# Moving one stream of weight loads from SyncE's queue to GpSimd's

## The chip, the cores and the metric

The kernel runs on one core of a Trainium2 chip. A core has engines that run their own instruction streams and meet at semaphores: TensorE (PE in the profile; its weight loads are PEld), VectorE (DVE), ScalarE (ACT), GpSimd (POOL) and SyncE (SP), which here does nothing but issue DMAs. A DMA is issued by an engine's queue and carried out by the core's 16 DMA engines. The metric is device time in microseconds of one execution; each version is given as the median of several runs.

## The reference

The program is a small backbone of two layers over 256 latent tokens and 256 context tokens of width 1024, batch 1. Each layer has a half-step SwiGLU, a mixer (neighbourhood attention in layer 0, a short gated convolution in layer 1) and another half-step SwiGLU. Every sub-layer is modulated by vectors that are computed from a conditioning vector:

```python
for i in range(DEPTH):
    m = (s_c @ ada_w[i] + ada_b[i]).reshape(B, N_MOD, 1, D)     # latent tokens
    mc = (s_cc @ ada_w[i] + ada_b[i]).reshape(N_MOD, D)         # context tokens
    x = half_step_ffn(x, m[:, 0], m[:, 1], m[:, 2], ffn_w_in[i, 0], ffn_w_out[i, 0], ...)
    if ctx_in:
        ctx = half_step_ffn(ctx, mc[0], mc[1], mc[2], ffn_w_in[i, 0], ffn_w_out[i, 0], ...)
    hx = modulate(x, m[:, 3], m[:, 4])
    ...
```

with `half_step_ffn` = LayerNorm(alpha x + 0.5 gate f(x (1 + scale) + shift)), f(h) = (silu(a) u) w_out, (a, u) = h w_in, and D_FF = 2816. `ada_w` has 2 x 1024 x 9216 fp32 numbers, 75 MB: nine blocks of 1024 x 1024 a layer, each of which gives one modulation vector from a vector-matrix product. These are the modulation weights.

## The kernel before

Everything is fp32. For TensorE each fp32 operand is split into a rounded high part and a low rest, and a product takes three matmuls (high x high, high x low, low x high). A unit of FFN weights comes into a raw buffer (`w1r` for the input matrix, `w2r` for the output matrix, tag `wr`, four buffers, issued by SyncE at L202), ScalarE rounds it into `w1h` or `w2h` (L207) and VectorE subtracts to get `w1l` or `w2l` (L210). Each split goes in two halves. A raw buffer is free again when VectorE's second half is done.

Three stages matter here.

1. **Start** (to about 46 us). The first two modulation blocks, needed at once, are loaded through SyncE (`start_load`, L577) and multiplied on TensorE, while the first inputs come.
2. **First FFN** (about 46 to 401 us), for latent and context tokens together. It goes in three parts over the hidden width (4, 4 and 3 panels). In each, `f0_mm` makes the chunks of the hidden layer (TensorE L671), `f0_gate` takes silu on ScalarE (L680), multiplies on VectorE (`sil`, L681), rounds on ScalarE (`gh`, L109) and subtracts on VectorE (`gl`, L110); then `out_gemm` multiplies with w_out (TensorE L161, L162, L164).
3. **The rest**: attention, and from about 600 us the other FFNs and the convolution.

Beside the first FFN runs a **background stream**: 11 of the modulation blocks, in seven groups. The first three groups have one block each, used for two vectors (latent and context); the other four have two blocks each, used for one. The generator `ada` loads a block in eight pieces of 128 x 1024 (512 KB, tile `ar`, tag "ar", three buffers, L300), 88 in all, and VectorE accumulates each piece, times the conditioning value of its partition, in two halves into `acc` (L291 for the first piece of a block, L293 after that). So a piece costs four VectorE instructions in the first three groups and two in the others. Right after a piece is loaded its accumulation is traced. When a group's blocks are done, eight small matmuls with a matrix of ones sum over the partitions (L324), VectorE adds a bias (L325, from a tile that GpSimd clears once, L312, and SyncE loads, L315), and the rows go to a scratch in memory (L327).

`set_background` starts the stream with a rate; `tick`, called after every few matmuls as the program is traced, advances it by that rate, and `drain` (L763) finishes it at the end of the first FFN. Three more streams, set at L1095, L1098 and L1160, load the remaining modulation blocks through the same `ada` later, 40 pieces in all.

The order of TensorE's instructions is written by hand (`manual_schedule`). The order on the other engines is planned from priorities and readiness when the program is built; each engine then runs its instructions in that fixed order. An instruction waits, where it stands in its queue, for the semaphores that it needs: a load for its buffer, an accumulation for its load. What stands behind it in the same queue waits too. Before the change SyncE's queue holds all loads of the first FFN, weights and modulation pieces alike, and the small stores. GpSimd has clearing at the start, two small instructions a LayerNorm (L397, L398) and the additions of a bias to the attention mask (L872).

Of the kernel before, what the change touches and what calls it, by code (L numbers as in the profile page):

```python
# [16 lines left out]
P = 128  # L17
D = 1024
# [49 lines left out]
def backbone_kernel(  # L68
# [6 lines left out]
    nc = tc.nc  # L75
    sync = nc.sync
# [11 lines left out]
    w_early = [0]  # L88
    ext = [1, 0]
    ada_late = [0]  # L90

    def nm(s):
        uid[0] += 1
        return f"{s}_{uid[0]}"
# [10 lines left out]
    def tpb(s="tp"):  # L105
        return bank("tp", s)
# [28 lines left out]
    def bg_step():  # L135
        with tc.high_priority(offset=-ada_late[0]):
            if next(background[0], 0) == 0:
                background[0] = None
# [14 lines left out]
    def drain():  # L153
        while background[0] is not None:
            bg_step()
# [116 lines left out]
    def ada(vecs):  # L272


        acc = {}

        def accumulate(l, m, k, w):
            with ExitStack() as st:
                for i in gate_ins:
                    st.enter_context(tc.issue_after(i.ins))  # L280
                for i, vec in enumerate(vecs):
                    if vec[:2] != (l, m):
                        continue
                    if k == 0:
                        a = hp.tile([P, D], F32, tag="acc", bufs=2, name=nm("acc"))
                        acc[i] = [a[:, 0:512], a[:, 512:D]]
                    sc = cst[:, k, vec[2]:vec[2] + 1]
                    for h in range(2):
                        src, a = w[:, h * 512:(h + 1) * 512], acc[i][h]
                        if k == 0:  # L290
                            nc.vector.tensor_scalar(a, src, sc, None, op0=ALU.mult)  # L291
                        else:
                            nc.vector.scalar_tensor_tensor(out=a, in0=src, scalar=sc, in1=a,  # L293
                                                           op0=ALU.mult, op1=ALU.add)

        loaded = []
        for l, m in dict.fromkeys((l, m) for l, m, _ in vecs):
            for k in range(KC):
                w = hp.tile([P, D], F32, tag="ar", bufs=3, name=nm("ar"))
                sync.dma_start(w, ada_w[l, k * P:(k + 1) * P, m * D:(m + 1) * D])  # L300
                loaded.append((l, m, k, w))
                if len(loaded) > (ADA_LAG if gate_ins else 0):
                    accumulate(*loaded.pop(0))
                yield 1
        while loaded:
            accumulate(*loaded.pop(0))
            if loaded:
                yield 1
        n = 2 * len(vecs)
        if not bias_rows:  # L310
            bias_rows.append(hp.tile([P, 512], F32, tag="adab", name=nm("adab")))
            nc.gpsimd.memset(bias_rows[0], 0.0)  # L312
        bt = bias_rows[0]
        for i, (l, m, v) in enumerate(vecs):
            sync.dma_start(bt[64 * i:64 * i + 64:32], ada_b[l, m * D:(m + 1) * D].rearrange("(a b) -> a b", b=512))  # L315
        yield 1
        yield 1
        yield 1
        rows = hp.tile([P, 512], F32, tag="adar", name=nm("adar"))
        ps = tpb("ada")  # L320
        for i in range(len(vecs)):
            for h in range(2):
                j = 2 * i + h
                nc.tensor.matmul(ps[32 * j:32 * j + 32, :], ones, acc[i][h], start=True, stop=True)  # L324
        nc.vector.tensor_tensor(out=rows[:32 * n], in0=ps[:32 * n], in1=bt[:32 * n], op=ALU.add)  # L325
        for i, (l, m, v) in enumerate(vecs):
            sync.dma_start(scr[l][v, m * D:(m + 1) * D].rearrange("(a b) -> a b", b=512),  # L327
                           rows[64 * i:64 * i + 64:32, :])
        yield 1
# [3 lines left out]
    def stream(*groups):  # L333
        for g in groups:
            yield from ada(g)
            made[0] += 1
# [424 lines left out]
                     nk, order, evac, "w2", wrow0=k0 * P))  # L761

    drain()  # L763

    def s2t(s):
        return sp.tile([P, 512], F32, tag="s2", bufs=S2, name=nm(s))
# [345 lines left out]
    w = sc_w_in[0]  # L1112
# [103 lines left out]
```

## Time and profile before

| what | value |
|---|---|
| median of 3 runs | 1267.73 us (1265.61 to 1269.18) |
| the profiled execution's own time | 1268.98 us |
| its span, first to last instruction | 1267.2 us |
| mean granted TensorE clock | 0.997 |
| DMA, whole span | 268.59 MB, 212 GB/s |
| SyncE's queue (q1) | 267.48 MB, 67.4% of the 16 engines' time |
| DMA share, 46 to 176 us and 176 to 366 us | 0.73 and 0.78 |

The profile has one page and several views that can be cut to a stretch of time: busy time by stage, groups of instructions, who waited for whom and how long, one tile's instructions, and the timeline. In rows of groups and timelines stand the source line, the engine, the operation, what is written and read (names of tiles without buffer numbers), the shapes, the count, and in brackets or after a bar the idle time of the engine just before, with what ended it. "SPq" is SyncE's queue of issues. Times are microseconds from the start of the span, durations in groups nanoseconds.

### The profile page before, as it was taken

How to read it: one execution, taken by the hardware profiler on the slowest of the kernel's cores; microseconds unless marked ns; L12 is line 12 of the kernel's file. 1: busy time of each engine (PE TensorE's matmuls, PEld its weight loads, DVE VectorE, ACT ScalarE, POOL GpSimd, SP SyncE). 2: the span in 40 equal slices, each digit the busy share in tenths (PEclk: the TensorE clock that was granted, in tenths of full speed). 3: DMA queues.
4: the chain of work that ended last, by engine and by line, in shares of the span. 5: the costliest groups of instructions: out<-in, count | busy, mean ns of one | idle time of the engine just before them, and what ended most of it. 6: DMA issues, size and time to landing. Idle time of an engine off the chain costs nothing.

```text
span 1267.2 us, 17289 instructions
## 1 busy us (share of the span) xinstructions
PE 1245.2 (98%) x5910; PEld 1004.7 (79%) x5910; DVE 955.2 (75%) x1685; ACT 590.1 (47%) x1152; POOL 42.1 (3%) x71
## 2 busy tenths in 40 slices
PE   8999999999999999989999999999999999999997
PEld 5787778787778778767888788888788887888786
DVE  4698987588888867889898646988546788977546
ACT  2433132312326456687755535645435744655431
POOL 0000000000001111111000000000000000000000
PEclk9999999999999999999999999999999999999999
DMA  9977678497862654564899645898645764886641
GB/s 301 305 220 232 186 239 301 161 309 236 286 229 84 197 111 77 107 136 126 266 326 326 234 145 180 267 324 281 224 149 168 232 217 133 260 284 187 217 158 57
DMA packets 202776, 268.59 MB, mean 212 GB/s; under 512 B 30090, under 2 KB 149362, under 8 KB 202688
## 3 DMA queue, kind: packets, MB, share of 16 engines
q1 hardware_dynamic: 202652, 267.48, 67.4%
q8 instruction: 46, 0.75, 0.2%
q14 instruction: 42, 0.34, 0.1%
q10 hardware_dynamic: 36, 0.02, 0.0%
HBM read 265.27 MB, written 2.17 MB: 211 GB/s over the span
## 4 chain that ended last, share of the span: by engine, by line
PE 87%; DMA 4%; DVE 4%; ACT 3%; SPq 1%; issue 1%; POOL 0%; DVEq 0%; ACTq 0%; POOLq 0%
PE f L671 18%; PE w L161 17%; PE w L164 17%; PE w L162 17%; PE wc L161 2%; PE wc L164 2%; PE wc L162 2%; DMA ar<-in_ada_w_dram 2%; PE gT L482 1%; PE wkv L161 1%; PE wkv L162 1%; PE wkv L164 1%; PE S L956 1%; DMA bias<-in_na_rpb_dram 1%; PE wo L161 1%
## 5 line engine op out<-in xcount | busy, mean ns | idle before, releaser
L207 ACT ACTIVATE w1h<-w1r 128x512 fp32r<-128x512 f32 (+1 forms) x352 | 200.2, 620 | 173.7 <-PE w L164 68.4
L210 DVE TENSOR_TENSOR w1l<-w1r,w1h 128x512 fp32r<-128x512 f32 (+1 forms) x352 | 222.8, 678 | 46.7 <-ACT w1h L207 45.1
L161 PE MATMUL w<-w1h,hTh 128*128 128x512 f32 x528 | 209.4, 397 | 0.9 <-ACT hTh L109 0.9
L162 PE MATMUL w<-w1l,hTh 128*128 128x512 f32 x528 | 206.0, 390 | 0.2 <-DVE w1l L210 0.2
L293 DVE SCALAR_TENSOR_TENSOR acc<-ar,cst,acc 128x512 f32<-128x512 f32 x266 | 185.3, 745 | 14.6 <-DMA ar<-in_ada_w_dram 14.4
L161 PE MATMUL w<-w2h,gh 128*128 128x512 f32 (+1 forms) x446 | 173.5, 390 | 1.4 <-ACT gh L109 1.4
L162 PE MATMUL w<-w2l,gh 128*128 128x512 f32 (+1 forms) x446 | 172.1, 386 | 0.0
L210 DVE TENSOR_TENSOR w2l<-w2r,w2h 128x512 fp32r<-128x512 f32 x176 | 114.2, 687 | 72.6 <-ACT w2h L207 71.3
L207 ACT ACTIVATE w2h<-w2r 128x512 fp32r<-128x512 f32 x176 | 101.5, 624 | 144.3 <-PE w L164 105.7
L164 PE MATMUL w<-w1h,hTl 128*128 128x512 f32 x528 | 163.2, 390 | 0.3 <-DVE hTl L110 0.2
L671 PE MATMUL f<-h0h,w1h 128*128 128x512 f32 x352 | 137.2, 394 | 0.6 <-ACT w1h L207 0.6
L671 PE MATMUL f<-h0h,w1l 128*128 128x512 f32 x352 | 136.1, 390 | 1.1 <-DVE w1l L210 1.1
L164 PE MATMUL w<-w2h,gl 128*128 128x512 f32 (+1 forms) x446 | 136.2, 386 | 0.0
L671 PE MATMUL f<-h0l,w1h 128*128 128x512 f32 x352 | 136.1, 390 | 0.0
L161 PEld LDWEIGHTS w<-w1h,hTh 128*128 128x128 f32 x528 | 99.2, 188 | 23.8 <-ACT hTh L109 1.7
L164 PEld LDWEIGHTS w<-w1h,hTl 128*128 128x128 f32 x528 | 98.9, 188 | 22.4 <-DVE hTl L110 1.5
L162 PEld LDWEIGHTS w<-w1l,hTh 128*128 128x128 f32 x528 | 99.2, 188 | 20.2 <-DVE w1l L210 0.6
L161 PEld LDWEIGHTS w<-w2h,gh 128*128 128x128 f32 x446 | 83.8, 188 | 20.9 <-issue 2.5
L164 PEld LDWEIGHTS w<-w2h,gl 128*128 128x128 f32 x446 | 83.3, 188 | 17.2 <-DVE gl L110 0.2
L162 PEld LDWEIGHTS w<-w2l,gh 128*128 128x128 f32 x446 | 83.8, 188 | 16.6
L671 PEld LDWEIGHTS f<-h0h,w1h 128*128 128x128 f32 x352 | 65.8, 188 | 19.7 <-issue 5.0
L671 PEld LDWEIGHTS f<-h0h,w1l 128*128 128x128 f32 x352 | 65.9, 188 | 14.7 <-DVE w1l L210 1.6
(182 smaller groups left out, 1705.9 us busy)
## 6 DMA issues: line engine op xcount, KB each, us to landing
w1r<-in_ffn_w_in_dram SPq DMA_DIRECT2D x340, 256.0 KB
ar<-in_ada_w_dram SPq DMA_DIRECT2D x128, 512.0 KB
w2r<-in_ffn_w_out_dram SPq DMA_DIRECT2D x88, 512.0 KB
ar<-in_ada_w_dram SPq DMA_DIRECT2D x32, 256.0 KB
wkvr<-in_na_w_qkv_dram SPq DMA_DIRECT2D x32, 256.0 KB
wcr<-in_sc_w_in_dram SPq DMA_DIRECT2D x32, 256.0 KB
wqr<-in_na_w_qkv_dram SPq DMA_DIRECT2D x8, 512.0 KB
bias<-in_na_rpb_dram SPq DMA_DIRECT2D x64, 64.0 KB
```

The source lines that it names most:

```text
L161: nc.tensor.matmul(ps, lh, rh, start=first and i == 0, stop=False)
L162: nc.tensor.matmul(ps, lh, rl, start=False, stop=False)
L164: nc.tensor.matmul(ps, ll, rh, start=False, stop=last and i == n - 1)
L207: nc.scalar.activation(hi[:, a:a + m // W_HI], raw[:, a:a + m // W_HI], AF.Copy)
L210: nc.vector.tensor_tensor(out=lo[:, a:b], in0=raw[:, a:b], in1=hi[:, a:b].bitcast(F32), op=ALU.subtract)
L293: nc.vector.scalar_tensor_tensor(out=a, in0=src, scalar=sc, in1=a, op0=ALU.mult, op1=ALU.add)
L482: nc.tensor.transpose(ps[:, j * 256 + i * P:j * 256 + (i + 1) * P], g[:, j * P:(j + 1) * P], ident)
L671: nc.tensor.matmul(ps, w, hT0[k][part == 1], start=(k == part == 0), stop=(k == KC - 1 and part == 1))
L956: nc.tensor.matmul(banks[i], (qh, qh, ql)[f][ps, qs], (kh, kl, kh)[f][ps, :], start=f == 0, stop=f == 2)
```

## The change

The queue on which `ada` issues its loads becomes a variable. It is GpSimd's while the first FFN is traced and SyncE's from the end of the first FFN's `drain` on. So the 88 loads of the stream beside the first FFN are issued by GpSimd; the start's loads (L577), the 40 later pieces, the stream's bias loads and stores, and all weights stay on SyncE. What is loaded, into which buffers, and what is computed stay the same.

```diff
@@ -88,6 +88,7 @@
     w_early = [0]
     ext = [1, 0]
     ada_late = [0]
+    ada_queue = [nc.gpsimd]
 
     def nm(s):
         uid[0] += 1
@@ -297,7 +298,7 @@
         for l, m in dict.fromkeys((l, m) for l, m, _ in vecs):
             for k in range(KC):
                 w = hp.tile([P, D], F32, tag="ar", bufs=3, name=nm("ar"))
-                sync.dma_start(w, ada_w[l, k * P:(k + 1) * P, m * D:(m + 1) * D])
+                ada_queue[0].dma_start(w, ada_w[l, k * P:(k + 1) * P, m * D:(m + 1) * D])
                 loaded.append((l, m, k, w))
                 if len(loaded) > (ADA_LAG if gate_ins else 0):
                     accumulate(*loaded.pop(0))
@@ -761,6 +762,7 @@
                      nk, order, evac, "w2", wrow0=k0 * P))
 
     drain()
+    ada_queue[0] = sync
 
     def s2t(s):
         return sp.tile([P, 512], F32, tag="s2", bufs=S2, name=nm(s))
```

## The prediction

> **What bounds the kernel now.** I read the page first, then the busy times of the stages, then who waits for whom in the first FFN, and last the timelines of the one place there at which TensorE stands still.
>
> ```profile
> span 1267.2 us, 17289 instructions
> PE 1245.2 (98%) x5910; PEld 1004.7 (79%) x5910; DVE 955.2 (75%) x1685; ACT 590.1 (47%) x1152; POOL 42.1 (3%) x71
> ```
>
> TensorE is busy for 98% of the span: all its idle time is 1267.2 - 1245.2 = 22.0 us, and no change of a load can bring more than that. Where those 22 us lie is in the stage table (stretch, length, then busy us and instructions of PE, PEld, DVE, ACT, POOL, granted clock, DMA share, GB/s):
>
> ```profile
> 46.00:176.00 130.00, 130.00 (x588) 104.93 (x588) 117.94 (x193) 41.38 (x74) 0.00 (x0) 1.00 0.73 226
> 176.00:366.00 190.00, 190.00 (x850) 154.49 (x847) 150.76 (x239) 54.37 (x94) 0.00 (x0) 1.00 0.78 262
> 366.00:411.00 45.00, 43.62 (x210) 34.78 (x209) 37.35 (x73) 21.70 (x48) 3.32 (x8) 1.00 0.33 104
> 411.00:600.00 189.00, 183.09 (x956) 144.38 (x955) 149.56 (x313) 122.47 (x267) 28.13 (x35) 0.99 0.53 124
> 600.00:1267.20 667.20, 658.71 (x3021) 539.95 (x3019) 480.48 (x824) 337.46 (x645) 9.32 (x18) 1.00 0.68 221
> ```
>
> The stream runs from 46 to 366 us, and there TensorE has no gap at all. VectorE is the second engine: 117.94 of 130 us, then 150.76 of 190, so it stands 51.3 us in these 320. GpSimd does nothing there. The whole idle time of TensorE between 45 and 420 us is one wait:
>
> ```profile
> PE w L161 <- ACT gh L109: 1.4, 1, 1.4
> ```
>
> So **the stage in which the change works can give 1.4 us at most**. What SyncE's queue waits for in this stretch, the row of the stream's loads (shortest, median and longest issue in ns), and what VectorE waits for:
>
> ```profile
> SPq L300 <- DVE acc L293: 102.2, 68, 3.4
> SPq L202 <- DVE w1l L210: 49.3, 30, 6.1
> ```
> ```profile
> L300 SPq DMA_DIRECT2D ar<-in_ada_w_dram x88: 323/340/612, 46.5 to 359.4; - x88
> ```
> ```profile
> DVE acc L293 <- DMA ar<-in_ada_w_dram: 14.4, 18, 1.8
> ```
>
> The 88 loads of the stream hold SyncE's queue for 102.2 us, because each needs a buffer (there are three) that VectorE frees with its last accumulation; weight loads (L202) stand behind them. And VectorE stood 18 times, 14.4 us in all, for such a load: the stream is bound by its three buffers and the time a load takes to land.
>
> **The change part by part.** *Issue.* SyncE loses 88 issues of 0.34 us (median of the row above), 30 us, and the 102.2 us of waits; GpSimd gets both. A load is no earlier by that: it still waits for the same accumulation. GpSimd has no other work from 46 to 366 us (0.00 in the table), its statistics come after the last load at 359.4, so nothing queues behind the waiting loads; the one memset of the stream's bias tile depends on no load. If the planner put that memset behind a waiting load, the bias load on SyncE would wait a few us; I cost it at nothing, since VectorE uses the bias only after eight loads' accumulations.
>
> *What SyncE gains.* Only the weights ahead of the one stall matter. SyncE:
>
> ```profile
> 344.30 5.85 SPq L300 DMA_DIRECT2D ar<-in_ada_w_dram  x4
> 350.25 0.39 SPq L202 DMA_DIRECT2D w2r<-in_ffn_w_out_dram  x1
> 351.92 7.79 SPq L300 DMA_DIRECT2D ar<-in_ada_w_dram  x4
> 359.76 0.94 SPq L202 DMA_DIRECT2D w2r<-in_ffn_w_out_dram  x2
> ```
>
> VectorE, ScalarE and TensorE around it:
>
> ```profile
> 347.70 1.28 DVE L210 TENSOR_TENSOR w2l<-w2r,w2h 128x512 fp32r<-128x512 f32 x2
> ...
> 350.48 1.42 DVE L293 SCALAR_TENSOR_TENSOR acc<-ar,cst,acc 128x512 f32<-128x512 f32 x2
> ...
> 357.94 2.74 DVE L293 SCALAR_TENSOR_TENSOR acc<-ar,cst,acc 128x512 f32<-128x512 f32 x4 [0.52 <-DMA ar<-in_ada_w_dram]
> 361.06 1.41 DVE L293 SCALAR_TENSOR_TENSOR acc<-ar,cst,acc 128x512 f32<-128x512 f32 x2 [0.38 <-DMA ar<-in_ada_w_dram]
> ...
> 364.38 1.41 DVE L293 SCALAR_TENSOR_TENSOR acc<-ar,cst,acc 128x512 f32<-128x512 f32 x2 [0.70 <-DMA ar<-in_ada_w_dram]
> ...
> 366.32 0.68 DVE L681 TENSOR_TENSOR sil<-sil,f 128x512 f32<-128x512 f32 x1
> ```
> ```profile
> 365.68 1.92 ACT L207 ACTIVATE w2h<-w2r 128x512 fp32r<-128x512 f32 x3 [3.59 <-DMA w2r<-in_ffn_w_out_dram]
> 367.50 0.61 ACT L109 ACTIVATE gh<-sil 128x512 fp32r<-128x512 f32 x1
> ```
> ```profile
> 368.17 0.50 PE L161 MATMUL w<-w2h,gh 128*128 128x512 f32 x1 [1.38 <-ACT gh L109]
> ```
>
> There are four raw weight buffers, loaded and split in turn; that of the load issued at 359.76 was free when the pair of splits at 347.70 ended, at 348.98. The load was issued 10.8 us later, behind four stream loads. It landed at about 365.7, where ScalarE stops waiting (3.59 us). The product (sil, L681) ends at 366.32 + 0.68 = 367.00, and ScalarE rounds it (gh) only at 367.50, since the late w2h pieces stand in front. With the weights on a free queue the w2h pieces are done before and gh can start at 367.00: **0.5 us gained**. The other 0.88 us of the stall remain, because sil itself stands behind accumulations that wait for stream loads. If those waits went too, the whole 1.38 would go: that is the floor of this term.
>
> *What the stream pays.* How long a load issued by GpSimd takes to land isn't in this trace. On SyncE, the quickest load that VectorE waited for, and a slow one:
>
> ```profile
> 333.02 0.34 SPq L300 DMA_DIRECT2D ar<-in_ada_w_dram  x1
> ```
> ```profile
> 336.62 1.42 DVE L293 SCALAR_TENSOR_TENSOR acc<-ar,cst,acc 128x512 f32<-128x512 f32 x2 [1.11 <-DMA ar<-in_ada_w_dram]
> ```
>
> Loads and accumulations go in the same order, so this is 3.60 us; the first of the four from 351.92 was waited for until 357.94, 6.02 us, with 512 KB of weights issued just before it. Call the change of the landing time x. Downwards x is -2.4 us, if all of 6.02 - 3.60 is queueing behind weights and goes; upwards I take the same 2.4, a load that shares the 16 DMA engines from start to end. The nearest row for the issue itself is GpSimd's own work:
>
> ```profile
> L872 POOL TENSOR_TENSOR bias<-bias,wmask 128x256 f32<-128x256 f32 x32 | 26.9, 841 | 141.8 <-DMA bias<-in_na_rpb_dram 111.4 <-DVE pT L110 10.8 <-PE qT L933 10.4
> ```
>
> 0.84 us for an instruction there against 0.34 us for an issue on SyncE: **I take x = +0.5 us**, the row nearest to what changes (who issues), with both ends kept for the range. [...]
>
> What does x cost? In the last stretch each load starts when the third before it is consumed, and the waits at 357.94, 361.06 and 364.38 show that landing is what limits it. The load waited for at 364.38 took its buffer from the one waited for at 357.94, that one from one consumed at 350.48: three links, each later by x, so sil is late by 3x = 1.5 us. gh then starts at 367.00 + 1.5 = 368.50 instead of 367.50. **Sum: 3 x 0.5 - 0.5 = +1.0 us** at this place, which the path then carries on: TensorE is full from there to 411 us. In the earlier stretches the cover holds: loads for two vectors (up to 176 us) are consumed at VectorE's pace, none of their accumulations waited (cut to 176 to 366 us, the view of VectorE's waits still has all 18), and after 176 us VectorE's waits for other engines absorb small delays.
>
> Span 1267.2 + 1.0 = 1268.2. The profiled execution took 1268.98 us, 1.8 around its span and 1.25 over the median of the three runs, so for a median I add the same 1.0: **1268.7 us**.
>
> **The rivals.** *Late landings decide (slower).* The same mechanism with x large. A difference of 0.3%, 3.8 us, is about what a measurement of this kernel can tell from no change; 3x - 0.5 reaches it at x = 1.43 us. At x = 2 this place gives 5.5, and a second opens:
>
> ```profile
> 253.68 0.68 DVE L681 TENSOR_TENSOR sil<-sil,f 128x512 f32<-128x512 f32 x1
> ...
> 255.61 0.68 DVE L110 TENSOR_TENSOR gl<-sil,gh 128x512 fp32r<-128x512 f32 x1
> ```
> ```profile
> 257.19 0.62 PE L164 MATMUL w<-w2h,gl 128*128 128x512 f32 x2
> ```
>
> Here gl ends at 256.29 and TensorE wants its half at 257.19 + 0.23 = 257.4: 1.1 us of cover against one link, so +0.9. In all +6.4, 1274.1 us; at the end x = 2.4 it is 7.2 - 0.5 + 1.3 = 8.0, 1275.7. For it: the stream has no spare buffer and waits already. Against it: without weights ahead of it in the queue, the 6.02 us load gets quicker.
>
> *GpSimd's issues slow VectorE (slower).* While GpSimd works on tiles in attention, the same split takes longer than later:
>
> ```profile
> L210 DVE TENSOR_TENSOR wkvl<-wkvr,wkvh 128x512 fp32r<-128x512 f32 x24 | 18.5, 807 | 1.1 <-ACT wkvh L207 1.1
> ```
> ```profile
> L210 DVE TENSOR_TENSOR w1l<-w1r,w1h 128x512 fp32r<-128x512 f32 x171 | 108.8, 683 | 21.9 <-ACT w1h L207 21.0
> ```
>
> That is 24 x 0.124 = 3.0 us over the 32 GpSimd additions, 0.1 us each. In the FFN, where about four times as much of VectorE's time goes to instructions with two tiles from SBUF, it could be 0.4 us for each of 88 loads, 35 us against 51.3 us of slack: ten loads in the last stretch give +4; up to 176 us, 27 loads would take 11 of the 12.06 us of slack, and as part of that slack is waiting for others I put a third of it, 4, on TensorE. That makes 1275.7 us. [...]
>
> *A luckier plan (faster).* Only TensorE's order is written by hand; the order on the others is planned, and another queue can shift it everywhere. Outside the stream TensorE stands for 5.9 us (411 to 600) and 8.5 us (from 600). The whole 1.38 and half of the 5.9 would give 1267.7 - 4.3 = 1263.4 us. Nothing in the profile points to it.
>
> *The move doesn't free the weights.* All loads share the same 16 DMA engines (busy 73 to 78%), so weights issued earlier may land no earlier. Then the 0.5 gained is missing and the 1.5 stay: 1269.2 us, no difference to be told either. [...]
>
> **How the numbers follow.** My forecast, no difference that can be told, has 0.48; not freed 0.07; late landings 0.26; slowed VectorE 0.07; a luckier plan 0.12. Faster by over 0.3% is 0.12, within 0.55, slower 0.33. The range reaches up over both slower cases to 1276.5 and down to 1264.3, the whole 1.4 us of the stall less the spread of the runs (1265.61 is 2.1 under their median); below lies most of the lucky plan, above a tail of the slower ones, together under 0.2. The forecast's own range is 1266.3 to 1271.5.
>
> **What would show it.** Right: TensorE's idle time from 46 to 411 us stays under 4 us, the load of w2 weights that was issued at 359.76 goes out near 349, and gh starts right behind sil. Wrong: VectorE's waits for stream loads far over 14.4 us with TensorE waiting for sil, gh or gl at 256 and 366 us (the late landings); L293 over 745 ns or L210 over 683 ns in the stream (the port); TensorE's idle time moved by more than 2 us outside the first FFN (the plan).

## The result, and the profile after

| | before | after |
|---|---|---|
| median | 1267.73 us (1265.61 to 1269.26, 5 runs) | 1280.74 us (1279.45 to 1281.88, 5 runs) |
| the profiled execution's own time | 1268.98 us | 1279.45 us |
| its span | 1267.2 us | 1277.7 us |

The ratio is 1.0103 (95% interval 1.009 to 1.0117): slower by 13 us, outside the range of the prediction. Line numbers of the changed kernel, and of all experiments, are higher by 1 from L91 on and by 2 from L764 on.

The page of the changed kernel, span and busy times:

```profile
span 1277.7 us, 17341 instructions
PE 1247.4 (98%) x5910; PEld 1007.1 (79%) x5910; DVE 954.6 (75%) x1685; ACT 590.2 (46%) x1152; POOL 88.3 (7%) x159
```

TensorE works 2.2 us longer on the same 5910 instructions, and its idle time went from 22.0 to 1277.7 - 1247.4 = 30.3 us. The stage table (columns as in the prediction):

```profile
46.00:176.00 130.00, 127.32 (x572) 103.14 (x571) 116.50 (x191) 40.94 (x73) 12.66 (x24) 1.00 0.69 216
176.00:366.00 190.00, 189.92 (x849) 153.22 (x848) 146.11 (x233) 56.41 (x97) 32.09 (x61) 1.00 0.78 261
366.00:411.00 45.00, 40.40 (x176) 31.50 (x175) 34.88 (x65) 13.46 (x31) 2.42 (x7) 0.92 0.32 96
...
1267.20:1277.70 10.50, 0.00 (x0) 0.00 (x0) 3.85 (x8) 0.00 (x0) 1.06 (x2) 0.65 0.13 50
```

TensorE, without a gap from 46 to 366 us before, now misses 2.7 us in the first row. Between 366 and 411 us it misses 4.6 us where it missed 1.4, and there the granted clock is 0.92 instead of 1.00. TensorE's waits from 45 to 420 us (total, times, longest):

```profile
PE w L162 <- ACT gh L110: 3.9, 1, 3.9
PE xT L618 <- DVE mcol L647: 1.4, 1, 1.4
PE f L672 <- DVE w1l L211: 1.3, 1, 1.3
PE w L163 <- DVE w2l L211: 0.7, 1, 0.7
```

One wait of 1.4 us has become four, 7.3 us. TensorE's order is the same in both kernels, so the two profiles can be laid over each other: how much later does the same matmul start? That gives the loss by place (worked out from the starts in the traces):

| | start, 49 to 68 us | 68 to 319 us | end of the stream, 319 to 372 us | from there to the last matmul | last matmul to end of span |
|---|---|---|---|---|---|
| after against before | +3.2 | 0.0 | +6.6 | -1.4 | +3.6 |

At 49 us the changed kernel's execution happened to be 1.5 us ahead; with that the sum is the 10.5 us between the two spans. The lead at 49 us and "from there to the last matmul" differ from one execution to the next: the first experiment below, nearly the kernel before, comes out 2.6 us ahead in the latter. Some 1.2 us of these 2.6 come between 558 and 561 us, where the clock had fallen to half for 3.4 us in the profiled execution of the kernel before and had not in that run. The stretch from 555 to 560 us of the kernel before:

```profile
555.00:560.00 5.00, 3.83 (x14) 2.44 (x15) 4.85 (x12) 3.56 (x8) 1.54 (x2) 0.74 0.75 109
```

So three places are left, and each needs its own explanation.

**The start.** VectorE:

```profile
47.66 1.67 DVE L292 TENSOR_SCALAR acc<-ar,cst 128x512 f32<-128x512 f32 x4 [2.75 <-DMA ar<-in_ada_w_dram]
49.24 0.15 DVE L646 COPY mcol<-mc 128x4 f32<-128x4 f32 x1
49.32 0.15 DVE L647 TENSOR_SCALAR mcol<-mc 128x4 f32<-128x4 f32 x1
50.69 0.75 DVE L294 SCALAR_TENSOR_TENSOR acc<-ar,cst,acc 128x512 f32<-128x512 f32 x1 [1.22 <-DMA ar<-in_ada_w_dram]
```

Two accumulations of the stream's first pieces stand on VectorE ahead of the start's last `mcol` and `h`, and wait 2.75 and 1.22 us for loads that GpSimd has only just issued. Before, the first accumulation stood at 57.77 us, behind that work.

**The end of the stream.** VectorE, the waits for the stream and the late product:

```profile
351.25 1.42 DVE L294 SCALAR_TENSOR_TENSOR acc<-ar,cst,acc 128x512 f32<-128x512 f32 x2 [2.21 <-DMA ar<-in_ada_w_dram]
...
360.46 1.42 DVE L294 SCALAR_TENSOR_TENSOR acc<-ar,cst,acc 128x512 f32<-128x512 f32 x2 [1.30 <-DMA ar<-in_ada_w_dram]
...
363.95 1.41 DVE L294 SCALAR_TENSOR_TENSOR acc<-ar,cst,acc 128x512 f32<-128x512 f32 x2 [1.48 <-DMA ar<-in_ada_w_dram]
365.95 2.74 DVE L294 SCALAR_TENSOR_TENSOR acc<-ar,cst,acc 128x512 f32<-128x512 f32 x4 [0.58 <-DMA ar<-in_ada_w_dram]
...
372.34 0.68 DVE L682 TENSOR_TENSOR sil<-sil,f 128x512 f32<-128x512 f32 x1
```

VectorE's order is nearly that of before (one more split of w2, 0.6 us, stands ahead of `sil`), but the waits are longer. From 330 to 372 us (total, times, longest), before and after:

```profile
DVE acc L293 <- DMA ar<-in_ada_w_dram: 3.7, 6, 1.1
```
```profile
DVE acc L294 <- DMA ar<-in_ada_w_dram: 7.9, 6, 2.2
```

`sil`, at 366.32 us before, comes at 372.34: 6.0 us later, of which TensorE itself was 2.0 late at 322 us, so 4.0 are new, about what the waits grew by. TensorE:

```profile
369.35 0.50 PE L163 MATMUL w<-w2l,gh 128*128 128x512 f32 x1 [0.71 <-DVE w2l L211]
373.74 0.79 PE L162 MATMUL w<-w2h,gh 128*128 128x512 f32 x1 [3.88 <-ACT gh L110]
374.33 0.63 PE L163 MATMUL w<-w2l,gh 128*128 128x512 f32 x1
...
376.03 0.63 PE L163 MATMUL w<-w2l,gh 128*128 128x512 f32 x1
376.46 0.63 PE L162 MATMUL w<-w2h,gh 128*128 128x512 f32 x1
```

The waits here are 0.71 + 3.88 us against 1.38 before, +3.2. Behind them the matmuls start 0.43 us apart (376.03 to 376.46) where 0.23 is usual, until about 379.5 us. The same table cut finer:

```profile
370.00:375.00 5.00, 1.26 (x3) 0.95 (x4) 5.00 (x9) 0.63 (x1) 0.00 (x0) 0.77 0.66 172
375.00:380.00 5.00, 5.00 (x14) 3.92 (x14) 3.02 (x5) 0.00 (x0) 0.00 (x0) 0.55 0.78 245
```

The clock was granted at 0.55; the next 14 matmuls lose another 2.65 us.

**The program's end.** The instructions of the kernel's last line, shortest, median and longest in ns; first before, then after:

```profile
L1212 POOLq DRAIN  x3: 34/78/971, 1261.8 to 1266.9; - x3
L1212 SPq DRAIN  x3: 7/7/7, 1266.4 to 1266.7; - x3
```
```profile
L1214 POOLq DRAIN  x3: 40/102/8184, 1268.7 to 1277.4; - x3
L1214 SPq DRAIN  x3: 7/7/7, 1273.3 to 1277.1; - x3
```

When its last small instruction is done, GpSimd drains its queue. That took 0.97 us and takes 8.18. It starts at 1268.70 and ends at 1276.89, while SyncE, which had closed the program before, is done at 1273.3: 3.6 us in which the core waits for nothing but this.

### The profile page after: what moved, and what is told of

The parts are those of the page before. It is cut to its first block, busy times and chain, and to the rows that moved or that the text cites. A ratio compares the mean times of both kernels' runs of the same rounds, so it can differ in the third digit from the quotient of the medians.

```text
span 1277.7 us, 17341 instructions
## 1 busy us (share of the span) xinstructions
PE 1247.4 (98%) x5910; PEld 1007.1 (79%) x5910; DVE 954.6 (75%) x1685; ACT 590.2 (46%) x1152; POOL 88.3 (7%) x159
## 4 chain that ended last, share of the span: by engine, by line
PE 64%; issue 18%; DMA 9%; DVE 4%; ACT 3%; POOL 2%; SPq 0%; DVEq 0%; POOLq 0%; ACTq 0%
PE w L162 15%; PE w L165 15%; PE w L163 15%; DMA ar<-in_ada_w_dram 7%; PE wkv L162 2%; PE wkv L163 2%; PE wkv L165 2%; PE wc L162 2%; PE wc L165 2%; PE wc L163 2%; POOL ar L301 2%; PE gT L483 1%; DMA w1r<-in_ffn_w_in_dram 1%; DVE acc L294 1%; PE S L958 1%
## 5 line engine op out<-in xcount | busy, mean ns | idle before, releaser
L294 DVE SCALAR_TENSOR_TENSOR acc<-ar,cst,acc 128x512 f32<-128x512 f32 x266 | 186.1, 745 | 23.7 <-DMA ar<-in_ada_w_dram 23.6
```

## The experiments

Each ran beside the kernel before on the same chip; ratios are to that. The last column is the drain of GpSimd, the three before it the shifts defined above.

| run | loads on GpSimd | ratio (95%) | start | end of the stream | last matmul to end | drain |
|---|---|---|---|---|---|---|
| after | 88 | 1.0103 (1.009 to 1.0117) | +3.2 | +6.6 | +3.6 | 8.18 |
| e1_one_small | 1 | 1.0003 (0.9994 to 1.0012) | 0.0 | -0.2 | +0.1 | 1.06 |
| e2_no_first | 80 | 1.0066 (1.0051 to 1.0081) | 0.0 | +6.3 | +3.0 | 7.53 |
| e3_no_last | 72 | 1.0064 (1.0051 to 1.0078) | +4.7 | -0.1 | +2.3 | 6.88 |
| e4_only_last | 16 | 1.004 (1.0024 to 1.0056) | 0.0 | +5.0 | +0.1 | 2.30 |
| e9_middle | 48 | 1.0003 (0.9993 to 1.0014) | 0.0 | -0.1 | +0.4 | 4.92 |

**One small load.** The load of `srow` (12 KB) goes through GpSimd, everything else through SyncE.

```diff
-    ada_queue = [nc.gpsimd]
+    ada_queue = [sync]
...
-    sync.dma_start(srow, sc_conv[0].rearrange("j (k p) -> (j k) p", p=P))
+    nc.gpsimd.dma_start(srow, sc_conv[0].rearrange("j (k p) -> (j k) p", p=P))
```

> The kernel before, with one load of 12 KB (srow, L1105), far from any wait, issued by GpSimd instead of SyncE. Theory A (a fixed price at the end of the program): as soon as GpSimd's queue has carried one load, GpSimd's drain at L1214 lasts about 8 us as in the changed kernel (8.18 us) and the span grows by about 3.5 us; the time is 1271 us, ratio 1.0028. Theory B (the drain is paid per load): 1/88 of it, so a drain under 0.2 us and 1267.7 us. Both: TensorE's stall near 366 us stays at 1.4 us.

Theory A was wrong. The drain is 1.06 us, 0.09 more than with no load, and the time did not change. With the other runs it is a line: 0.97 + 0.082 us a load gives 2.28, 6.87, 7.53 and 8.19 us for 16, 72, 80 and 88 loads, and 2.30, 6.88, 7.53 and 8.18 were measured. SyncE's own end covers it up to about 4.6 us.

**Without the first group, without the last, the last alone.** The line that issues the stream's loads, with GPS = (1, 2, 3, 4, 5, 6), (0, 1, 2, 3, 4, 5) and (6,):

```diff
-                ada_queue[0].dma_start(w, ada_w[l, k * P:(k + 1) * P, m * D:(m + 1) * D])
+                (nc.gpsimd if ada_queue[0] is not sync and made[0] in GPS else sync).dma_start(w, ada_w[l, k * P:(k + 1) * P, m * D:(m + 1) * D])
```

> The changed kernel with the stream's first group (8 of 88 loads) back on SyncE's queue. Theory A (the planner puts VectorE's first accumulations into the start because their loads go out early on GpSimd, and TensorE pays 1.5 us for it there): TensorE at 55 us is where the kernel before has it, the time falls by 1.5 us against the changed kernel, ratio to before 1.009, if nothing later takes it back. Theory B (the start only moves slack, and the waits at 366 us decide): TensorE is 1.5 us earlier at 55 us, and its stall near 366 us is longer by the same, ratio unchanged at 1.010.

> The changed kernel with the stream's last group (16 of 88 loads) back on SyncE's queue. Theory A (the late landings of the last group make gh late): TensorE's stall near 366 us falls from 3.9 to about 1.4 us and the granted clock behind it stays at 1.00 instead of 0.55; of the 10.5 us between the two profiled spans about 5 remain (1.5 from the start, 3.5 at the end), ratio 1.004. Theory B (the delay comes from the earlier groups and is only carried to this place): the stall stays over 3 us and the ratio at 1.010.

> The kernel before with only the stream's last group (16 of 88 loads) on GpSimd's queue. Theory A (last group late): stall of about 4 us near 366 us, clock under 0.8 behind it, GpSimd's drain of 8 us at the end; about 5 + 3.5 us more than before, ratio 1.007. Theory B (the delay comes from the earlier groups): stall 1.4 us, only the 3.5 us at the end, ratio 1.003.

By place, theory A held in all three; two of the sizes did not. Without the first group the start loses nothing, and the end of the stream loses as much as with it. Without the last group the waits of the start are all that is left; TensorE's waits from 45 to 420 us in that run:

```profile
PE xT L618 <- DVE mcol L647: 3.0, 1, 3.0
PE f L672 <- DVE w1l L211: 1.2, 1, 1.2
PE w L162 <- ACT gh L110: 1.2, 1, 1.2
```

The start was worth more than the 1.5 us that I had set: 3.2 and 4.7 us in these profiles, and the ratio fell by 0.0037 without it, 4.7 us, of which 0.7 is the drain of eight loads fewer. That is why e3_no_last kept 1.0064 and not 1.004. The last group alone makes the wait for `gh` 3.9 us and takes the clock down behind it (0.70 from 370 to 375 us), 5 us in all, the largest of the three losses; its drain of 2.30 us is covered, so that the ratio is 1.004 and not 1.007.

**Whose fault is the start?** All 88 loads stay on GpSimd, as early as in the changed kernel; VectorE's accumulations of the first two are made to issue behind the first `sil`.

```diff
-    gate_ins = []
+    gate_ins = []; g0 = []
...
-                for i in gate_ins:
+                for i in gate_ins + (g0[:1] if made[0] == 0 and k < 2 else []):
...
-        nc.vector.tensor_tensor(out=t, in0=t, in1=bk[1], op=ALU.mult)
+        g0.append(nc.vector.tensor_tensor(out=t, in0=t, in1=bk[1], op=ALU.mult))
```

> The changed kernel, all 88 loads on GpSimd's queue as early as there, but VectorE's accumulations of the first two loads are made to issue behind the first product of the gates (sil, L682), as in the kernel before. Theory A (the start's loss is VectorE's order: accumulations that wait for loads stand ahead of the start's mcol): TensorE loses nothing between 46 and 59 us (2.8 us in the changed kernel), the waits for mcol and w1l are gone, and the time falls to that of the run with the first group on SyncE, 1276.3 us, ratio 1.007. Theory B (the start's loss comes from the early loads themselves, which share the DMA engines with the start's weights): the wait for w1l stays, and with it 1.3 of the 2.8 us; ratio 1.009.

1276.08 us, ratio 1.0059 (1.0045 to 1.0072). TensorE loses nothing at the start, so it was VectorE's order, not the early loads. Why the planner chose that order when the queue changed was not looked at. TensorE's waits:

```profile
PE w L162 <- ACT gh L110: 4.0, 1, 4.0
PE w L163 <- DVE w2l L211: 0.5, 1, 0.5
PE f L672 <- DVE w1l L211: 0.2, 1, 0.2
```

**The clock.** 17 matmuls whose result nobody uses, directly ahead of the one that waits for `gh` (the edit is written out over several lines here); in e6_fill in the changed kernel, in e12_fill_behind in the one above.

```diff
     def mmu(ps, ops, first, last):
+        fill_now = spin.pop() if spin else 0
         n = len(ops)
         for i, (lh, ll, rh, rl) in enumerate(ops):
+            if i == 1 and fill_now:
+                spare = tpb("spare")
+                for _ in range(fill_now):
+                    nc.tensor.matmul(spare, ops[0][0], ops[0][2], start=True, stop=True)
             nc.tensor.matmul(ps, lh, rh, start=first and i == 0, stop=False)
...
         nk = len(gT)
+        spin[:] = [17, 0, 0] if fh == 2 else []
```

> The changed kernel with 17 more matmuls of 0.23 us (3.9 us, into a spare bank, their result is not used) on TensorE directly ahead of the matmul that waits 3.9 us for gh. Theory A (the granted clock falls because TensorE stood still for 3.9 us): the clock stays at 1.00 from 374 us on, the matmuls go on at 0.23 us, and the time falls by 2.6 us although work was added; ratio 1.008. Theory B (the clock falls for another reason, such as the work itself, or TensorE only pays the wait): nothing gained, ratio 1.010 or more.

> The run e5_acc_behind (no loss at the start) with the 17 matmuls ahead of the one that waits for gh. Theory A (the clock falls because TensorE stood still): clock 1.00 behind the place, and the 14 matmuls after it take 0.4 us more than in the kernel before instead of 1.7 us; the time is 1.3 us under that run, ratio 1.005. Theory B (the clock falls for another reason): the clock falls all the same, and the ratio stays at 1.006 or rises.

The stage table of e6_fill, behind the wait:

```profile
375.00:380.00 5.00, 4.81 (x21) 3.33 (x20) 4.96 (x9) 0.63 (x1) 0.00 (x0) 1.00 0.76 218
380.00:385.00 5.00, 5.00 (x24) 3.88 (x23) 3.50 (x12) 0.00 (x0) 0.00 (x0) 1.00 0.45 158
```

The clock stays at 1.00, and the 14 matmuls behind the place lose 0.43 us instead of 2.65 (0.44 instead of 1.70 in the second pair): the clock fell here because TensorE stood still. The time does not show it: 1280.04 us, ratio 1.0095 (1.008 to 1.0109) against 1.0103, and 1276.48 us, 1.0068 (1.0053 to 1.0084) against 1.0059. Some 1.3 to 2.2 us are about what these intervals can tell, and both profiles lose more than their partners ahead of the place: e12_fill_behind 0.5 us from 319 to 322 us, e6_fill 1.1 us there and 1.6 us more at the start. There its clock fell, though no gap there was longer than 2.92 us (the last section comes back to it):

```profile
51.77 0.41 PE L618 MATMUL xT<-ident,x 128*128 128x128 f32 x2 [2.92 <-DVE mcol L647]
```
```profile
50.00:55.00 5.00, 3.23 (x13) 2.70 (x14) 3.68 (x10) 3.28 (x8) 0.53 (x1) 0.82 0.78 271
```

As a gain this stays unproven.

**Only the middle.** GPS = (1, 2, 3, 4), with 8, 8, 16 and 16 loads. SyncE keeps the first group and the last two (the expectation names the first two by mistake).

> Only the stream's four middle groups (48 of 88 loads) on GpSimd's queue, the first two and the last on SyncE's (first group, and the two from 216 us on). Theory A (the whole loss sits in three places, the start, the end of the stream and the program's end, and each has its own condition): no loss at the start, the stall near 366 us at 1.4 us, GpSimd's drain 0.97 + 0.082 x 48 = 4.9 us (the line through the drains of the runs so far), which SyncE's own end covers up to 4.6 us; in all +0.3 us, ratio 1.000. Theory B (every load through GpSimd costs its share of the 13 us): 48/88 of it, 7 us, ratio 1.0056.

Theory A: 1267.56 us in both kernels. Loads that VectorE does not wait for with TensorE behind it cost nothing here (ratio 1.0003).

**Why do the last loads land late?** With the last group on GpSimd, either its path is slow, or the weights, no longer held up in one queue, now run beside the stream and share the DMA engines with it. Two runs move the weight loads too, by the weights' issue in `wunit`; e7_both_last has the last group on GpSimd, e8_swap_last the whole stream on SyncE.

```diff
-                sync.dma_start(rv[:, :, c:c + src.shape[2]], src)
+                (nc.gpsimd if made[0] == 6 else sync).dma_start(rv[:, :, c:c + src.shape[2]], src)
```

> As the run with only the last group of the stream (16 loads) on GpSimd, but the weight loads of that stretch go through GpSimd's queue too, in one order with the stream as SyncE had it before. Theory A (GpSimd's path itself makes a load land late): the stall near 366 us stays near 3.9 us and the time at 1272.5 us, ratio 1.004. Theory B (the stream's loads land late because the weights on the other queue run beside them and take half of the DMA engines): with one queue the order of before is back, the stall falls to about 1.4 us, the clock stays at 1.00, and the ratio is 1.000 to 1.001.

> The reverse: the whole stream on SyncE as before, and the weight loads of the last group's stretch on GpSimd's queue. Theory A (GpSimd's path makes a load land late): the stream's loads are quick, SyncE's have nothing ahead of them, sil is early, and the stall near 366 us is at most 1.4 us; ratio at most 1.001. Theory B (two queues side by side share the DMA engines, whichever holds the stream): the stream's loads land late again, stall 3 us or more, ratio 1.003 to 1.005.

Read by the times, 1.0044 (1.003 to 1.0058) and 1.0013 (1.0003 to 1.0024), GpSimd's path would be the cause. But the traces show that the edit missed: the stream's generator is through before the last weights are traced, so the condition no longer held for them. SyncE's queue in e7_both_last and in e8_swap_last:

```profile
341.64 12.87 SPq L203 DMA_DIRECT2D w2r<-in_ffn_w_out_dram  x3
```
```profile
352.39 0.38 SPq L203 DMA_DIRECT2D w2r<-in_ffn_w_out_dram  x1
353.82 7.95 SPq L301 DMA_DIRECT2D ar<-in_ada_w_dram  x4
361.94 0.38 SPq L203 DMA_DIRECT2D w2r<-in_ffn_w_out_dram  x1
```

The last three w2 loads are on SyncE in both: beside the stream in the first, in one queue with it in the second. Where it matters, at the end of the stream, these two are e4_only_last and the kernel before over again, and they don't decide the question. With the condition mended:

```diff
-                sync.dma_start(rv[:, :, c:c + src.shape[2]], src)
+                (nc.gpsimd if made[0] >= 6 and ada_queue[0] is not sync else sync).dma_start(rv[:, :, c:c + src.shape[2]], src)
```

> The last group of the stream (16 loads) and all weight loads of the same stretch (w1 and w2, to the end of the first FFN) through GpSimd's queue, in one order as SyncE had them before. Theory A (GpSimd's path itself makes a load land late): the stall near 366 us stays at 3 us or more, with the clock falling behind it; ratio 1.004. Theory B (two queues side by side share the DMA engines): the order of before is back, the stall falls to 1.4 to 2 us, ratio 1.000 to 1.002. GpSimd's drain for some 30 loads, 3.4 us by the line of the runs so far, is covered in both.

> The reverse of it: the stream all on SyncE as before, and all weight loads of the last group's stretch on GpSimd's queue, beside it. Theory A (GpSimd's path): the stream's loads are quick, nothing stands ahead of them on SyncE, and the stall near 366 us is at most 1.4 us; ratio at most 1.001. Theory B (sharing): VectorE waits for the stream's loads as long as with the last group on GpSimd (7.4 us from 330 to 372 us, 3.7 before), and the stall is 3 us or more; ratio 1.003 to 1.005.

The swap, with the stream on SyncE, has the whole loss: 1273.02 us, ratio 1.004 (1.0025 to 1.0055), +5.8 us at the end of the stream. TensorE, and SyncE's queue, where nothing but the stream is left:

```profile
367.68 0.50 PE L163 MATMUL w<-w2l,gh 128*128 128x512 f32 x1 [0.98 <-DVE w2l L211]
372.07 0.79 PE L162 MATMUL w<-w2h,gh 128*128 128x512 f32 x1 [3.89 <-ACT gh L110]
```
```profile
342.72 20.82 SPq L301 DMA_DIRECT2D ar<-in_ada_w_dram  x9
```

VectorE's waits for the stream from 330 to 372 us are 8.3 us, against 7.4 with the last group on GpSimd and 3.7 before. The load that SyncE issues at 342.72 us, just after two weight loads that GpSimd issued at 340.46 and 342.33, is waited for until 350.69, 7.97 us; in the kernel before the same load took 3.98 (342.38 to 346.36). So weights beside the stream are enough, with the stream on SyncE's queue too. In every run with two queues one of them is GpSimd's; two others were not tried.

With all in GpSimd's one queue, e13_one_queue, the time is nearly back: 1268.96 us, ratio 1.001 (1.000 to 1.002), +2.2 us at the place. But its trace is less clear than its time. VectorE from 330 to 372 us and TensorE from 45 to 420 (total, times, longest):

```profile
DVE acc L294 <- DMA ar<-in_ada_w_dram: 8.0, 6, 3.1
```
```profile
PE w L162 <- ACT gh L110: 3.1, 1, 3.1
```

VectorE waits for the stream as long as with two queues, and the stall of 3.1 us is what theory A had set; only the time and the clock, which stays at 1.00, fit theory B. The order of before is not back either: two weight loads (341.14 and 342.35 us) stand directly ahead of the stream's load at 343.09, and that one is waited for until 350.12, 7.03 us. Later loads are quicker than with two queues (the fourth and third from the end, issued at 355.16 and 358.00 us, take 4.43 and 4.35 us to their accumulations; in the changed kernel 7.02 and 7.09). So the run agrees with weights beside or ahead of the stream as the cause, but what of its 2.2 us is GpSimd's path and what the order of its queue is left open.

**A fourth buffer.** The stream's tile "ar" gets four buffers, paid for by two of the 38 activation buffers; e10_four_behind on top of e5_acc_behind, e11_four_sync with everything on SyncE.

```diff
-NACT = 38
+NACT = 36
...
-                w = hp.tile([P, D], F32, tag="ar", bufs=3, name=nm("ar"))
+                w = hp.tile([P, D], F32, tag="ar", bufs=4, name=nm("ar"))
...
-        return hp.tile([P, D], F32, tag="ar", bufs=3, name=nm("ar"))
+        return hp.tile([P, D], F32, tag="ar", bufs=4, name=nm("ar"))
```

> The changed kernel with VectorE's first accumulations behind the first product of the gates (as in the run e5_acc_behind) and a fourth buffer for the stream's loads, paid for with two fewer of the 38 activation buffers. Theory A (the last stretch is late because a load through GpSimd lands later than three buffers cover): the stall near 366 us is at most 1.4 us, the clock stays at 1.00, and only GpSimd's drain is left, 3.5 us; 1271 us, ratio 1.0028. Theory B (the lateness does not hang on the buffers): stall near 4 us, ratio 1.006.

> The kernel before (everything on SyncE's queue) with the fourth buffer, and two fewer activation buffers. If three buffers bound the stream there too, TensorE's stall of 1.38 us near 366 us goes, and the time falls by up to 1.4 us (ratio 0.999), less than can be told for sure; if that stall hangs on SyncE's order of weights, it stays and the ratio is 1.000.

e10_four_behind: 1270.92 us, ratio 1.0031 (1.0018 to 1.0043), the end of the stream -0.1, the wait for `gh` 0.9 us, and only the drain left (+3.6 behind the last matmul). By these ratios the order at the start takes 0.0044 of the 0.0103 (5.6 us), the buffer 0.0028 (3.5 us), and 0.0031 (3.9 us) stay. Each ratio is known to some 0.0013 only, and by place the profiles give 3.2, 6.6 and 3.6 us for the same three: that there are three parts is shown, how large each of the first two is is not.

e11_four_sync is **faster than both kernels**: 1265.99 us, ratio 0.9987 (0.9978 to 0.9997). Its stage row:

```profile
366.00:411.00 45.00, 45.00 (x219) 36.30 (x218) 35.59 (x70) 21.96 (x51) 3.32 (x8) 1.00 0.26 83
```

TensorE has no gap left there, and is 1.6 us earlier behind the place than before.

## Why the prediction was wrong

- **What bounds the kernel** held: that place could give 1.4 us at most, and with the fourth buffer TensorE is 1.6 us earlier behind it.
- **Issue** held. An issue takes GpSimd 0.53 us, nothing queued behind it, and the bias tile's clearing disturbed nothing.
- **What SyncE gains** was right as an event and wrong as a gain. The weights were freed:

```profile
343.35 14.32 SPq L203 DMA_DIRECT2D w2r<-in_ffn_w_out_dram  x4
```

  The load that went out at 359.76 us, the third of these, goes out at 354.77 and the last by 357.7, and `gh` starts right behind `sil` (372.34 + 0.68 = 373.02; 373.05). But by e14_swap the freed weights are what makes the stream late. Before, one queue held most of them back: they waited behind loads that waited for buffers.

- **"I take x = +0.5 us, the row nearest to what changes (who issues)" is the step that failed.** What mattered was not who issues but what runs beside a load. Two of the loads that VectorE waited for, GpSimd's issues (the accumulations at 351.25 and 363.95 are above):

```profile
345.48 0.53 POOL L301 DMA_DIRECT2D ar<-in_ada_w_dram  x1 [3.99 <-DVE acc L294]
...
356.93 0.53 POOL L301 DMA_DIRECT2D ar<-in_ada_w_dram  x1 [2.00 <-DMA ar<-in_ada_w_dram]
```

  The second took 7.02 us; the same load took 6.02 before (351.92 to 357.94). The first took 5.77; before, it was issued and waited for at

```profile
342.38 0.32 SPq L300 DMA_DIRECT2D ar<-in_ada_w_dram  x1
```
```profile
346.36 1.41 DVE L293 SCALAR_TENSOR_TENSOR acc<-ar,cst,acc 128x512 f32<-128x512 f32 x2 [0.16 <-DMA ar<-in_ada_w_dram]
```

  3.98 us. So x is 1.0 and 1.8 us there, and GpSimd issues 0.27 us later after a buffer is freed (0.30 us against 0.03). The issue by itself was not the price: of the 88 loads on GpSimd the quickest landed after 3.7 us, about the 3.60 of the quickest that the prediction read on SyncE. Nor is x one number for three links, as 3x - 0.5 has it: the load of the third link, waited for at 364.38 us before, is the last of the stream, and its accumulation (369.81 us after) waits for nothing any more. The loads that made `sil` late are others in part, those accumulated at 339.26, 351.25, 360.46, 363.95 and 365.95 us. That 3 x 1.4 - 0.5 = 3.7 us comes near the 4.0 by which `sil` is late is luck. The upper end, "a load that shares the 16 DMA engines from start to end", comes nearest to what the runs show, a load that takes longer with weights beside it (7.97 us against 3.98 in e14_swap); I had kept it for the range and taken the middle from the wrong row.
- **"In the earlier stretches the cover holds"** was right from 68 to 319 us, to 0.0 us, the place at 256 us included, and wrong for the first two loads. That the planner would place work by the new queue stood in the prediction only as a lucky plan. It put VectorE to wait ahead of the start: the same mechanism with the other sign, worth 3.2 to 4.8 us in the profiles.
- **Two terms were missing**: GpSimd's drain, 3.6 us, and the clock behind a stall, up to 2.65 us. The drain has no row in the profile of before, where GpSimd issues no load. The clock has one: there TensorE's longest wait between 45 and 420 us is 1.38 us, but behind 555 us the clock fell (0.74 in the row shown above, 0.99 in the prediction's row from 411 to 600 us), so that a stall could cost more than its length was to be read from it.
- **The rivals.** Late landings did decide, but even their end of 1275.7 us was too low without the other three terms. What the prediction calls the port, VectorE slowed by GpSimd's issues, did not show: the accumulations (L294) last 745 ns on average, as before, and the splits of `w1` from 46 to 366 us 684 ns in both kernels. That the slowing would grow with VectorE's time on instructions with two tiles from SBUF, to 0.4 us a load, was my estimate, and no run shows it. "The move doesn't free the weights" is refuted. The idea behind it, that all loads share the same engines, fits the loss at the end of the stream: e14_swap has +5.8 us there without GpSimd's path for the stream, with a load that takes 7.97 us instead of 3.98.

## What to carry to other kernels

The queue that all loads shared was also a brake here: it kept bulk loads from running beside the loads that VectorE waited for (3.7 us of such waits from 330 to 372 us in the kernel before, 8.3 in e14_swap, where the weights ran beside the stream). Before splitting such a queue, ask which loads it holds back today, and what happens to the one on the path when they run beside it; where a stream waits for buffers, a further buffer is the first thing to try (here it took the wait for `gh` from 4.0 us in e5_acc_behind to 0.9 in e10_four_behind). A planner may order the consumers anew when a queue changes, as it did here (two accumulations ahead of the start's `mcol`, with waits of 2.75 and 1.22 us), so look at where it puts the first ones.

## What was not expected of the hardware

- GpSimd's drain at the program's end grew with the number of loads that it had issued, as 0.97 + 0.082 us a load from 0 to 88, although in the changed kernel the last of them landed some 900 us earlier. Past about 4.6 us it shows in the span here: a drain of 4.92 us comes with +0.4 us behind the last matmul (e9_middle), one of 8.18 us with +3.6.
- TensorE's granted clock fell behind gaps of 3.88 to 4.03 us (to 0.50 to 0.70 in the lowest five-microsecond row, six runs), each with a shorter wait of 0.4 to 1.0 us one matmul earlier, and did not fall behind gaps of 2.95 (e3_no_last) and 3.12 us (e13_one_queue; 1.00 in the rows from 365 to 380 us). But it did fall behind one of 2.92 us (e6_fill, 0.82 in the row from 50 to 55 us), and in the kernel before at 557.37 us behind gaps of 1.55 us and less. So the length of a single gap does not tell in these runs whether the clock falls.
- In the profiles of before and after the falls have lengths of 3.41 us (557.37 to 560.78 us before, 563.83 to 567.24 us after) and twice that (372.69 to 379.51 us after), each at 0.50, and their starts lie 706.56 us apart before (557.37 and 1263.92 us) and 191.15 and 706.56 us after (372.69, 563.83 and 1270.39 us), which is 207, 56 and 207 times 3.413 us. I cut both profiles from 46 us on into pieces of 3.413 us that end at those starts. In the piece just ahead of a fall TensorE stood idle for 0.46 (before), 0.85 and 0.57 (after) of the time, and for all of it at the program's end; in no other piece with the clock at 1.00 for more than 0.40. The gap of 3.88 us in the changed kernel is the 0.85. This was read from these two profiles and not tested by a run of its own, and why 2.92 us were enough in e6_fill and 3.12 us were not in e13_one_queue is left open.
